# Second attention's scores as whole-array products of stacked high and low parts, and three adaLN maps moved to the feed-forward parts

## The chip, the cores and the metric

The kernel runs on one core of one Trainium2 chip (trn2). The metric is the device time of one execution in microseconds. Five engines work side by side: TensorE multiplies matrices (its weight loads are shown as an engine of their own), VectorE and ScalarE work elementwise and read the results out of PSUM, GpSimd helps with elementwise work, and SyncE (SP) issues the DMA transfers.

## The reference, cut to what matters

A trunk of two layers over 1024 latent tokens and 256 context tokens, width 1024, 16 heads of 64. Layer 0 mixes tokens by neighbourhood attention, layer 1 by sliding-window attention with 4 key and value heads (each serves 4 query heads), rotary positions and a sink logit for each head. Each layer ends with a gated feed-forward part with a convolution. Shift, scale and gate vectors ("adaLN maps", six for each layer, here v = 0 to 5) come from the condition vectors through one linear map.

```python
mod = silu_c @ w_mod[i] + b_mod[i]
sh1, sc1, gt1, sh2, sc2, gt2 = jnp.split(mod[:, None, :], 6, axis=-1)   # v = 0 .. 5
h = modulate(rmsnorm(x, g_attn[i]), sh1, sc1)
...
q = apply_rope(q, cos, sin)
k = apply_rope(k, cos, sin)
...
# sliding window: 128 queries see at most 384 latent keys (|i - j| <= 128) and all 256 context keys
s = jnp.einsum('...qngd,...knd->...ngqk', q, k) * (HEAD_DIM ** -0.5)
s = jnp.where(mask, s, NEG_INF)           # and a sink column
p = jax.nn.softmax(s, axis=-1)
...
x = x + gt1 * (o @ w_out)
h = modulate(rmsnorm(x, g_ffn[i]), sh2, sc2)
x = x + gt2 * conv_ffn(h, ...)
```

Layer 1 needs six maps for the latent tokens (r = 0) and only v = 0 and 1 for the context (r = 1), since the context's stream ends there.

## The kernel before, in words

Everything is float32. Large products are made as three products of the faster float32r kind, with each operand split in a high part (rounded by ScalarE) and a low part (the rest, by VectorE or GpSimd): high by high, low by high, high by low. A few products are made in plain float32.

The program is made stage by stage: first attention, its output projection, first feed-forward part (`ffn(0, ...)`), second attention, its output projection, second feed-forward part (`ffn(1, ...)`). In each stage a planner (`Sched`, line 61) is given operations with an engine (or two to choose from), an estimated duration, what they read and write, a key (smaller is earlier), and buffers to acquire and release (`caps` says how many there are of each kind). It simulates the engines and writes down the order of each engine's instructions; on the chip every engine then works strictly in that order. A key is a rank and no time to start. With `near=3.0` TensorE, after an operation marked as half-array ("t"), prefers another such one that is up to 3 keys later.

The second attention (from line 2326) works in four groups g of key and value heads. For each group, `plan_sw_qkv` makes for each tile tt of 128 tokens the projection (24 products of 384 columns), copies it out (`qraw`), normalises the heads, applies the rotation (`qn`, `qa`, `qb`, the last on GpSimd), transposes three 128x128 blocks into one PSUM bank ("pt"), and copies these out: two blocks of queries (each has two heads on 64 partitions each) into a tile `q`, and one block with the key head twice (on both halves of the partitions) into `kkl1`. Its key is 1.6 per tile, 16 per group. The context's keys go into `kkc1` in the same way (`plan_sw_ctx`). All of these are plain float32.

`plan_sw_su` then makes the attention for 128 queries j and a pair pr of heads, 64 such units in all. `plan_row_qk` multiplies 64 partitions of `q` with 64 partitions of the keys, for both heads side by side: the two heads lie on the two halves of TensorE's rows ("64*128" tiles in the profile). It acquires four PSUM banks of kind "s" at once: context scores and window scores of both heads; there are four. `plan_su` takes the scores' minimum against sink and mask on VectorE, the exponential on ScalarE, scales, transposes the probabilities ("pt" banks again) and copies them out; `plan_pv` multiplies with V for two pairs of heads at a time, in half-array tiles by columns ("128*64"). `plan_su` can also make its scores with `plan_split_qk`, as the first attention does: the operands are stacked, with the high part of a head's queries on one half of the partitions and the low part on the other, against keys that are held twice (high parts in one tile, low parts in another), so that two products over all 128 partitions make the whole score.

PSUM has eight banks here: 4 "s", 2 "pt", 2 "mm".

The maps of layer 1: `plan_mod1` (line 350), called in the first feed-forward part, makes v = 0 and 1 for both r. Each of its 64 dots (8 blocks x 2 maps x 2 r x 2 halves of the row) loads 128x512 of the weights into the one `mh` buffer (line 2033) and makes a dot on VectorE (`wmh` in the profile) with the c row, of which ScalarE makes a copy for each r and half. `plan_modv` (line 396), called in the second attention for v = 2 to 5, makes a dot of 128x1024 for each of 32 blocks (`wmt`), at keys 20 + 1.2 n.

`Oproj` (line 806) makes the output projection: `split` the high and low parts of the attention's output (`o0hi`, `o0lo` for the first 512 tokens, `o1hi`, `o1lo` for the rest), `weights` those of the weights, `project` the products. All wait (`gate`) for the projections of all eight tiles of the last group, as their buffers are those of the normalised input. `plan_oproj1` loads the residual x into the two buffers that held the context's normalised input (`hchi`, `hclo`).

Of the kernel before, what the change touches and what calls it, by code (L numbers as in the profile page):

```python
# [223 lines left out]
def trunk_kernel(ctx, tc, xtok, xseq, cc, crow, wmod, wmodt, bmod, gnorm, na_wqkv, na_gqk, na_bias, na_wo,  # L224
# [125 lines left out]
    def plan_mod1(sc, tile_, bank, key, step):  # L350

        crow = {}
        for r in range(2):
            for half in range(2):
# [10 lines left out]
                sc.op("act", t_actp(512), cp, reads=[ck + ("t",)], writes=[ck], key=key, acq=[("b", ck + ("p",), 2 * KT)], rel=[ck])  # L365
                for v in range(2):
                    for jt in range(KT):
                        st = {}
                        m = ("mh", r, v, jt)
                        raw = ("mh", r, half, v, jt)  # L370

# [6 lines left out]
                        def dot(e, st=st, r=r, half=half, v=v, jt=jt):  # L378
                            k = 24 + (2 * r + v) * KT + jt
                            a, b = small[:, k:k + 1], modc[:, 1, r, v, jt:jt + 1]  # L380
# [3 lines left out]
                        sc.op("dve", 0.7, dot, reads=[raw + ("here",), ck] + ([m + (0,)] if half else []), writes=[m + (half,)],  # L384
                              key=key, rel=[raw, ck + ("p",)])
                        key += step
        for v in range(2):
            def fin_(e, v=v):
                if v:
                    for r in range(2):  # L390
                        dve.scalar_tensor_tensor(out=modc[:, 1, r, v, :], in0=modc[:, 1, r, v, :], scalar=1.0, in1=gn[:, 1, 0, :],
                                                 op0=ALU.add, op1=ALU.mult)
            sc.op(*(("dve", 0.3) if v else ("x", 0.0)), fin_, reads=[("mh", r, v, jt, 1) for r in range(2) for jt in range(KT)],
                  writes=[("modc", v)], key=key)
# [140 lines left out]
    def plan_row_qk(sc, key, I, get, nl, psa, reads, rel):  # L535
        J = {}

        def mm(e):
            for h in range(2):
                J["sc", h], J["sl", h] = psa("s", F32), psa("s", F32)  # L540
            u = get()
            for t, x, n in (("sc", "kkc", TC), ("sl", "kk", nl)):
                for h in range(2):
                    a = slice(h * DH, h * DH + DH)
                    pe.matmul(J[t, h][:, :n], u["q"][a], u[x][a], start=True, stop=True)
        out = [I + (t, h) for h in range(2) for t in ("sc", "sl")]
        sc.op("pe", 0.207 + (TC + nl) * 4 / 2400.0, mm, kind="t", reads=reads, writes=out, key=key, acq=[("s", x, 1) for x in out],
              rel=rel)
        return J, I

    def plan_su(sc, key, I, units, groups, psa, wk, reads=()):
# [4 lines left out]
        if "s" not in units[0]:  # L556
            plan_split_qk(sc, key, J, K, units, psa, reads)
        for k in range(2):
            nl, sink = units[k]["nl"], units[k]["sink"]
            n = TC + nl  # L560
            if "s" in units[k]:
                Q, QI, hh = units[k]["s"]
                kc, kl, c0 = QI + ("sc", hh), QI + ("sl", hh), 0
                src_c, src_l = (lambda Q=Q, hh=hh: Q["sc", hh]), (lambda Q=Q, hh=hh: Q["sl", hh])
            else:
                kc, kl, c0 = K("sc"), K("sl", k), k * 256
                src_c, src_l = (lambda: J["sc"]), (lambda k=k: J["sl", k])
# [238 lines left out]
    class Oproj:  # L806
# [14 lines left out]
        def split(self, c, name, n, src, dst, key, reads, rel):  # L821
# [8 lines left out]
            g = self.c_gate if c == 2 else self.gate  # L830
# [23 lines left out]
        def project(self, dt, key, parts, evac):  # L854
# [3 lines left out]
            for kt in range(KT):  # L858
# [8 lines left out]
                sc.op("pe", 3 * t_pe(n), mm, reads=[("woh", dt), ("wol", dt)] + parts[kt] + self.gate, writes=[I], key=key,  # L867
# [494 lines left out]
    SRB, GB, MOD1 = 4, 3, 160  # L1362
# [3 lines left out]
    def ffn(l, opj, xt1, todo):  # L1366
# [665 lines left out]
        if not last:  # L2032
            plan_mod1(sc, lambda nm: fp.tile([P, 512], F32, tag="mh", name=nm, bufs=1), bank, MOD1, (KD - 120 - MOD1) / 64)
# [135 lines left out]
        def plan_ev(d, m, c, k, key, end=False):  # L2169
# [3 lines left out]
                reads=[("dn", d, m)], writes=[("xn", c, k)], key=key,  # L2173
# [157 lines left out]
    psa = ps_alloc(ps)  # L2331
    crow1 = fin.tile([P, D], F32, name="crow1")
    kkl1 = fin.tile([P, 2, T], F32, name="kkl1")
# [3 lines left out]
    PVT, SBUFS = "pt", 6  # L2337
    sc = Sched(dict(CAPS, pt5=6, pt2=3, qsq=1, q=10, S=SBUFS, s=4, qraw=3, qa=3, qn=3), near=3.0)
# [4 lines left out]
    KC = fin.tile([P, NKV, TC], F32, name="kkc1")  # L2343
    VC = [fin.tile([P, NKV, DH], F32, name=f"vc1{i}") for i in range(2)]

    def plan_sw_ctx(tt, key):
# [44 lines left out]
        sc.op("pe", 0.44, tr, reads=[K("k2")], writes=[K("pt")], key=key, acq=[("pt", K("pt"), 1)], rel=[K("k2")])  # L2391

        def kev(e):
            copy(e, KC[:, :, c * P:(c + 1) * P], J["pt"].rearrange("p (g k) -> p g k", g=NKV))
        sc.op(("act", "dve"), (t_actp(512), t_dve(512)), kev, reads=[K("pt")], writes=[("kC", c)], key=key, rel=[K("pt")])

    def plan_sw_qkv(n):
        g, tt = n // NT, ORDER[n % NT]
        key = n / NT * 16 + QKEY1
# [3 lines left out]
        nh, c0 = 5, 0  # L2403
# [3 lines left out]
        def cp(e):  # L2407
            J["raw"] = wk.tile([P, 384], F32, tag="qraw", name="qraw", bufs=3)
# [13 lines left out]
        def qn(e):  # L2422
            J["qn"] = wk.tile([P, 5, DH], F32, tag="qn", name="qn", bufs=3)
# [271 lines left out]
```

## Time and profile before

| | |
|---|---|
| median of 3 runs | 2730.73 us (2729.62 to 2731.26) |
| the profiled execution | 2731.01 us, span 2729.2 us |
| TensorE granted clock | 0.995 |
| second attention, about | 1604 to 2014 us of the span |
| score products in it | 1634.3 to 2002.0 us |
| dots of `plan_mod1` | 64, from 725.9 to 1286.8 us |
| dots of `plan_modv` in the second attention | 32, from 1662.2 to 1911.7 us |

Times in the profile are microseconds from the first instruction. A busy share is the share of time in which an engine has at least one instruction at work; TensorE's products overlap, and their ends are modelled, so the distance between two starts tells more than a length. A row of the timeline has the start, the length, the engine, the line (here always that of the helper that issues everything, L51), the operation, result and operands, the tile of the array and the shape, and how many there were. A row of one tile has the count, minimum, median and maximum duration in ns, first and last start, and the forms of a sample.

### The profile page before, as it was taken

How to read it: one execution, taken by the hardware profiler on the slowest of the kernel's cores; microseconds unless marked ns; L12 is line 12 of the kernel's file. 1: busy time of each engine (PE TensorE's matmuls, PEld its weight loads, DVE VectorE, ACT ScalarE, POOL GpSimd, SP SyncE). 2: the span in 40 equal slices, each digit the busy share in tenths (PEclk: the TensorE clock that was granted, in tenths of full speed). 3: DMA queues.
4: the chain of work that ended last, by engine and by line, in shares of the span. 5: the costliest groups of instructions: out<-in, count | busy, mean ns of one | idle time of the engine just before them, and what ended most of it. 6: DMA issues, size and time to landing. Idle time of an engine off the chain costs nothing. (4 is left out here: it accounts for less than half of the span.)

```text
span 2729.2 us, 42690 instructions
## 1 busy us (share of the span) xinstructions
PE 2680.4 (98%) x15168; PEld 2277.0 (83%) x15168; DVE 2290.8 (84%) x5063; ACT 1691.4 (62%) x3001; POOL 356.2 (13%) x520
## 2 busy tenths in 40 slices
PE   7999999999999999999999999999999999999999
PEld 5999999988899988888888887777678788888887
DVE  5988888888788899898886889899867988888767
ACT  6777777776455565656664557776654765656443
POOL 1211111122000000000010026455510000000000
PEclk8999999999999999999999999999999999999999
DMA  7343343344656744344475642233243233334655
GB/s 265 97 122 121 117 136 110 105 136 151 245 188 215 230 145 135 122 145 140 143 248 165 205 144 72 63 107 103 90 147 108 89 116 107 109 109 148 232 176 189
DMA packets 167005, 395.23 MB, mean 145 GB/s; under 512 B 36996, under 2 KB 44164, under 8 KB 166408
## 3 DMA queue, kind: packets, MB, share of 16 engines
q1 hardware_dynamic: 166792, 392.51, 44.1%
q8 instruction: 119, 1.95, 0.3%
q14 instruction: 94, 0.77, 0.1%
HBM read 325.46 MB, written 66.99 MB: 144 GB/s over the span
## 5 line engine op out<-in xcount | busy, mean ns | idle before, releaser
L51 ACT ACTIVATE whi<-wraw 128x512 fp32r<-128x512 f32 (+1 forms) x264 | 212.5, 805 | 148.3 <-PE uc L51 53.5
L51 DVE TENSOR_TENSOR wlo<-wraw,whi 128x512 fp32r<-128x512 f32 (+1 forms) x264 | 241.5, 915 | 33.5 <-ACT whi L51 31.5
L51 ACT ACTIVATE S<-S,m 128x640 f32<-128x640 f32 (+3 forms) x288 | 220.9, 768 | 68.2 <-DVE m L51 47.3
L51 PE MATMUL dn<-ghi,whi 128*128 128x512 f32 x616 | 240.0, 390 | 0.0
L51 PE MATMUL dn<-ghi,wlo 128*128 128x512 f32 x616 | 239.7, 389 | 0.0
L51 PE MATMUL dn<-glo,whi 128*128 128x512 f32 x616 | 239.7, 389 | 0.0
L51 ACT ACTIVATE whi<-s 128x1024 fp32r<-128x1024 f32 (+1 forms) x118 | 111.0, 942 | 182.6 <-PE uc L51 117.0
L51 POOL TENSOR_TENSOR qy<-qv,mhalf 128x4 f32<-128x4 f32 (+1 forms) x114 | 134.9, 1185 | 560.7 <-DVE qv L51 527.5
L51 PE MATMUL pt<-idr,S 128*128 128x128 f32 x1288 | 194.1, 278 | 14.1 <-DVE S L51 7.2
L51 PEld LDWEIGHTS pt<-idr,S 128*128 128x128 f32 x1288 | 151.5, 142 | 51.6 <-issue 11.8
L51 ACT ACTIVATE ghi<-graw 128x512 fp32r<-128x512 f32 x154 | 95.8, 629 | 142.2 <-PE dn L51 95.7
L51 ACT ACTIVATE pt<-pt 128x512 f32<-128x512 f32 (+2 forms) x263 | 136.5, 540 | 73.9 <-PE pt L51 72.0
L51 PE MATMUL mm<-whi,h0hi 128*128 128x384 f32 x512 | 179.9, 351 | 0.0
L51 PE MATMUL mm<-wlo,h0hi 128*128 128x384 f32 x512 | 172.0, 336 | 0.0
L51 DVE TENSOR_TENSOR glo<-graw,ghi 128x512 fp32r<-128x512 f32 x154 | 106.4, 699 | 73.4 <-ACT ghi L51 43.0
L51 DVE TENSOR_TENSOR wlo<-s,whi 128x1024 fp32r<-128x1024 f32 (+1 forms) x118 | 127.0, 1079 | 14.1 <-ACT whi L51 13.6
L51 PEld LDWEIGHTS dn<-ghi,whi 128*128 128x128 f32 x616 | 115.6, 188 | 24.3 <-issue 0.2
L51 PEld LDWEIGHTS dn<-glo,whi 128*128 128x128 f32 x616 | 115.6, 188 | 24.0
L51 PEld LDWEIGHTS dn<-ghi,wlo 128*128 128x128 f32 x616 | 115.6, 188 | 23.9
L51 PE MATMUL ua<-t12hi,whi 128*128 128x512 f32 x344 | 134.4, 391 | 0.9 <-ACT c L51 0.9
L51 PE MATMUL ua<-t12lo,whi 128*128 128x512 f32 x344 | 133.9, 389 | 0.0
L51 PE MATMUL ua<-t12hi,wlo 128*128 128x512 f32 x344 | 133.9, 389 | 0.0
(370 smaller groups left out, 8353.7 us busy)
## 6 DMA issues: line engine op xcount, KB each, us to landing
wraw<-in_w_up_dram SPq DMA_DIRECT2D x133, 512.0 KB, 3.8
wmt<-in_wmodt_dram SPq DMA_DIRECT2D x96, 512.0 KB, 4.1
wraw<-in_w_down_dram SPq DMA_DIRECT2D x44, 512.0 KB, 3.8
graw<-g_dram SPq DMA_DIRECT2D x44, 512.0 KB, 4.5
wraw<-in_w_down_dram SPq DMA_DIRECT2D x88, 256.0 KB, 3.1
graw<-g_dram SPq DMA_DIRECT2D x66, 256.0 KB, 2.8
wmh<-in_wmodt_dram SPq DMA_DIRECT2D x64, 256.0 KB, 3.3
slab<-in_na_wqkv_dram SPq DMA_DIRECT2D x32, 384.0 KB, 3.1
```

Source lines behind the costliest of these rows:

```text
L51: r = f(*a, **k)
```

## The change

1. Scores: `plan_row_qk` goes; `plan_sw_su` uses `plan_split_qk`. So queries and keys of this layer are split. `q` becomes four blocks (one for each head) with high and low parts on the two halves of the partitions, made by two ScalarE and two VectorE operations; the keys become `kkl1` and `kll1`, `kkc1` and `klc1`, by one ScalarE and one VectorE operation each. The transposes' bank is released after six readers instead of two.
2. Room: `q` has 5 buffers (8 uses) instead of 10 (2 uses). `qraw`, `qn` and `qb` move into the two buffers of the context's normalised input (`ring`), and the residual's load waits for the last group's transposes.
3. Keys: tile tt of group g has 16 g + 2 tt + 2.6 instead of 16 g + 1.6 (tt + 2).
4. Maps: v = 3 and 4 (r = 0) of layer 1 are made in the first feed-forward part by `plan_mod1`, which now takes a list of jobs: 96 dots of half a row instead of 64, from key 120 instead of 160 to the same end. v = 5 is made in the second feed-forward part: 16 dots. Only v = 2 stays in the second attention: 8 whole-row dots instead of 32.
5. Output projection of layer 1: the first half's `split` and the products wait for four tiles' projections instead of eight; the second half's splits for the other four.

```diff
-    def plan_mod1(sc, tile_, bank, key, step):
+    def plan_mod1(sc, tile_, bank, jobs, key, end):
-        crow = {}
-        for r in range(2):
+        crow, part = {}, {}
+        step = (end - key) / sum(2 * KT * len(vs) for _, vs in jobs)
+        for r, vs in jobs:
...
-                for v in range(2):
+                for v in vs:
...
-        if "s" not in units[0]:
-            plan_split_qk(sc, key, J, K, units, psa, reads)
+        plan_split_qk(sc, key, J, K, units, psa, reads)
...
-                for k in (2,) if c == 2 else (0, 1):
+                for k in (c,) if c == 2 or self.l else (0, 1):
...
-            g = self.c_gate if c == 2 else self.gate
+            g = self.c_gate if c == 2 else self.gate[4 * c:4 * c + 4] if self.l else self.gate
...
-    SRB, GB, MOD1 = 4, 3, 160
+    SRB, GB, MOD1 = 4, 3, 120
...
-        if not last:
-            plan_mod1(sc, lambda nm: fp.tile([P, 512], F32, tag="mh", name=nm, bufs=1), bank, MOD1, (KD - 120 - MOD1) / 64)
+        mh = lambda nm: fp.tile([P, 512], F32, tag="mh", name=nm, bufs=1)
+        plan_mod1(sc, mh, bank, *(([(0, [5])], KU + 100, KD - 120) if last else ([(0, [0, 1, 3, 4]), (1, [0, 1])], MOD1, KD - 120)))
...
-    kkl1 = fin.tile([P, 2, T], F32, name="kkl1")
+    kkl1, kll1 = [fin.tile([P, 2, T], F32R, name=nm) for nm in ("kkl1", "kll1")]
...
-    PVT, SBUFS = "pt", 6
-    sc = Sched(dict(CAPS, pt5=6, pt2=3, qsq=1, q=10, S=SBUFS, s=4, qraw=3, qa=3, qn=3), near=3.0)
+    PVT, SBUFS, QB1 = "pt", 6, 5
+    sc = Sched(dict(CAPS, pt5=6, pt2=3, qsq=1, q=QB1, S=SBUFS, s=4, qraw=3, qa=3, qn=3), near=3.0)
...
+    AREA = {}
+    def ring(i, a, n, bufs, m):
+        if i not in AREA:
+            AREA[i] = hpool.tile([P, 2048], F32, tag=("hchi", "hclo")[i], name=f"ring{i}", bufs=1)
+        return AREA[i][:, a + m % bufs * n:a + m % bufs * n + n]
...
-        key = n / NT * 16 + QKEY1
+        key = 16 * g + 2 * tt + 2.6 + QKEY1
...
-              acq=[("pt", K("pt"), 2)], rel=[K("a")])
-        kk = ("kk", g % 2, tt)
-        def kev(e):
-            copy(e, kkl1[:, g % 2, tt * P:(tt + 1) * P], J["pt"][:, 2 * P:3 * P])
-        sc.op(("act", "dve"), (t_actp(128), t_dve(128)), kev, reads=[K("pt")], writes=[kk], key=key, rel=[K("pt")])
-        def qev(e):
-            q = f["q"][tt] = fin.tile([P, 2, P], F32, tag="q", name="q", bufs=10)
-            copy(e, q.rearrange("p a b -> p (a b)"), J["pt"][:, :2 * P])
+              acq=[("pt", K("pt"), 6)], rel=[K("a")])
...
+        for x in range(2):
+            def qhi(e, x=x):
+                if x == 0:
+                    f["q"][tt] = fin.tile([P, 4, P], F32R, tag="q", name="q", bufs=QB1)
+                act.activation(qt(x, x), qp(x), AF.Copy)
+            def qlo(e, x=x):
+                dve.tensor_tensor(out=qt(1 - x, x), in0=qp(x), in1=qt(x, x).bitcast(F32), op=ALU.subtract)
...
-    for n in range(4 * KT):
+    for n in range(KT):
         plan_modv(sc, 1, 0, 2 + n // KT, n % KT, wmodt[1, 2 + n // KT, n % KT], lambda: crow1, MKEY + MSTEP * n, [("crow1",)])
...
-            sc.op("dma", 3.2, load, reads=op1.gate, writes=[("xc", k)], key=OKEY + k)
+            sc.op("dma", 3.2, load, reads=op1.gate + [("q1", NKV - 1, t, "pt") for t in range(8)], writes=[("xc", k)],
+                  key=OKEY + k)
```

More of the change, by code (lines that the diff above doesn't have):

```diff
@@ L533, in plan_split_qk @@
                       acq=[("s", K("sl", k), 1)], rel=units[k]["rel_l"])
[L535 to L549, printed above, removed]
     def plan_su(sc, key, I, units, groups, psa, wk, reads=()):
@@ L2342, in trunk_kernel @@
     SLAB0 = (("dve", "pool"), (0.87, 1.75))
-    KC = fin.tile([P, NKV, TC], F32, name="kkc1")
+    KC, KL = [fin.tile([P, NKV, TC], F32R, name=nm) for nm in ("kkc1", "klc1")]
     VC = [fin.tile([P, NKV, DH], F32, name=f"vc1{i}") for i in range(2)]
@@ L2436, in qb @@
         def qb(e):
[L2437 removed]
+            J["b"] = ring(0, 1152, 320, 2, nt).rearrange("p (h d) -> p h d", d=DH)
             for k, s, m in spans:
@@ L2479, in plan_sw_su @@
         nl, m0 = (hi - lo + 1) * P, P if j == 0 else 0
-        Q = plan_row_qk(sc, key, I, lambda: dict(q=f["q"][j][:, pr, :], kkc=KC[:, g, :], kk=kkl1[:, g % 2, ks]), nl, psa,
-                        [("q", g, j), ("kC", 0), ("kC", 1)] + [("kk", g % 2, t) for t in range(lo, hi + 1)], [("q", g, j)])
+        reads = [("q", g, j, x, z) for x in range(2) for z in range(2)] + [(n, c) for n in ("kC", "kD") for c in range(2)]
+        reads += [(n, g % 2, t) for n in ("kk", "kl") for t in range(lo, hi + 1)]
         for k in range(2):
@@ L2485, in get @@
             def get(hd=hd):
-                return dict(mask=bandt[:, m0:m0 + nl], sink=sink[:, 4 * g + hd:4 * g + hd + 1])
-            units.append(dict(nl=nl, sink=1, get=get, mask_key=[], s=Q + (k,)))
+                return dict(q=f["q"][j][:, hd, :], kkc=KC[:, g, :], klc=KL[:, g, :], kk=kkl1[:, g % 2, ks], kl=kll1[:, g % 2, ks],
+                            mask=bandt[:, m0:m0 + nl], sink=sink[:, 4 * g + hd:4 * g + hd + 1])
+            units.append(dict(nl=nl, sink=1, get=get, mask_key=[], rel_c=[("q", g, j)], rel_l=[("q", g, j)]))
         lst = [(8 + i, i * P, i * P) for i in range(2)] + [(b, *[TC + (b - lo) * P] * 2) for b in range(lo, hi + 1)]
@@ L2490, in plan_sw_su @@
                for t, a, b in lst]
-        f["half", pr] = plan_su(sc, key, I, units, [lst[i:i + 2] for i in range(0, len(lst), 2)], psa, wk)
+        f["half", pr] = plan_su(sc, key, I, units, [lst[i:i + 2] for i in range(0, len(lst), 2)], psa, wk, reads)
         if pr == 0:
@@ L2561, in plan_oproj1 @@
                 key = OKEY + 6 * (c - 1) + kt
-                sc.op("dma", 1.0, load, reads=[("od", kt // 2, 2 * c + i) for i in range(2)] + op1.gate, writes=[r], key=key, acq=[("raw", r, 2)])
+                sc.op("dma", 1.0, load, reads=[("od", kt // 2, 2 * c + i) for i in range(2)] + op1.gate[4 * c:4 * c + 4], writes=[r], key=key, acq=[("raw", r, 2)])
                 op1.split(c, (c, kt), 512, lambda c=c, kt=kt: R[c, kt][:, :512], lambda a, kt=kt: a[:, kt, :], key + 0.5, [r], [r])
```

74 lines of the change are left out of this document (45 added, 29 removed).

## The prediction

> **What bounds the kernel now.** I read the page first, then the busy times by stage, then who waited for whom on TensorE, then TensorE's timeline.
>
> ```profile
> span 2729.2 us, 42690 instructions
> PE 2680.4 (98%) x15168; PEld 2277.0 (83%) x15168; DVE 2290.8 (84%) x5063; ACT 1691.4 (62%) x3001; POOL 356.2 (13%) x520
> ```
>
> ```profile
> 850.00:950.00 100.00, 100.00 (x836) 100.00 (x835) 79.02 (x138) 54.14 (x81) 0.00 (x0) 1.00 0.74 232
> 1000.00:1300.00 300.00, 300.00 (x1325) 248.50 (x1324) 269.28 (x354) 181.83 (x215) 0.00 (x0) 1.00 0.40 135
> 1604.00:2014.00 410.00, 397.36 (x2681) 306.30 (x2681) 363.18 (x1195) 282.30 (x611) 219.88 (x400) 0.99 0.28 88
> 2150.00:2550.00 400.00, 399.31 (x1762) 330.32 (x1761) 334.41 (x395) 244.57 (x303) 0.00 (x0) 1.00 0.39 131
> ```
>
> The stage rows give TensorE, its weight loads, VectorE, ScalarE and GpSimd, then the granted clock. The first two rows lie in the first feed-forward part, the third is the second attention, the fourth is in the second feed-forward part. TensorE is at work without a hole in the feed-forward parts. In the second attention it stands idle for 410.00 - 397.36 = 12.6 us, and VectorE works for 363.2 of the 410. So the whole kernel goes at TensorE's pace: time is won where TensorE's stream gets shorter, and lost only where a wait opens in it. TensorE's own waits in the second attention, the three largest:
>
> ```profile
> PE pt L51 <- DVE S L51: 3.8, 4, 1.8
> PE pt L51 <- POOL qa L51: 3.5, 4, 1.3
> PE pt L51 <- ACT o0hi L51: 2.4, 1, 2.4
> ```
>
> They are single late arrivals in an order fixed beforehand, not one engine that is always late.
>
> **The score products.** All score products of this layer, first by count, then one stretch of TensorE's timeline (start, length, how many):
>
> ```profile
> L51 PE MATMUL s<-kkc,q x256: 376/480/793, 1634.3 to 2001.6; 64*128 64x256 f32 x128
> L51 PE MATMUL s<-kkl,q x256: 376/482/845, 1634.8 to 2002.0; 64*128 64x384 f32 x96, 64*128 64x256 f32 x32
> ```
>
> ```profile
> 1701.99 0.81 PE L51 MATMUL pt<-idr,S 128*128 128x128 f32 x6
> 1702.57 0.42 PE L51 MATMUL mm<-whi,h1hi 128*128 128x384 f32 x1
> ...
> 1704.52 0.33 PE L51 MATMUL mm<-whi,h1lo 128*128 128x384 f32 x1
> 1704.69 0.34 PE L51 MATMUL mm<-wlo,h1hi 128*128 128x384 f32 x1
> 1704.96 0.70 PE L51 MATMUL s<-kkc,q 64*128 64x256 f32 x4
> 1705.49 0.81 PE L51 MATMUL s<-kkl,q 64*128 64x384 f32 x4
> 1706.24 1.08 PE L51 MATMUL pt<-pt,vc 128*64 128x256 f32 x8
> ...
> 1709.13 0.70 PE L51 MATMUL s<-kkc,q 64*128 64x256 f32 x4
> 1709.67 0.60 PE L51 MATMUL s<-kkl,q 64*128 64x256 f32 x4
> 1710.20 0.87 PE L51 MATMUL pt<-idr,S 128*128 128x128 f32 x6
> 1710.83 0.42 PE L51 MATMUL mm<-whi,h1hi 128*128 128x384 f32 x1
> ```
>
> Four entries a pair of heads make 256 / 4 = 64 units; the forms (a sample, 96 to 32) say that three quarters, 48, have a window of 384 keys and 16 one of 256. The lengths overlap, so I price by the distance between starts. A unit with 384 keys takes 1706.24 - 1704.96 = 1.28 us, one with 256 takes 1710.20 - 1709.13 = 1.07. Around a unit lies more: the projection ahead of it takes 1704.96 - 1704.69 = 0.27 where its neighbour takes 0.17, so 0.10 to enter half-array tiles; and the six transposes behind one take 1710.83 - 1710.20 = 0.63 where six behind a projection take 1702.57 - 1701.99 = 0.58, so 0.05 after it. A unit that stands alone costs 1.43 or 1.22 us.
>
> The new form stands in this trace already: the first attention has it, with the same sizes.
>
> ```profile
> 308.39 0.28 PE L51 MATMUL s<-kkc,q 128*128 128x256 f32 x1
> 308.50 0.28 PE L51 MATMUL s<-klc,q 128*128 128x256 f32 x1
> ...
> 308.86 0.28 PE L51 MATMUL s<-kkl,q 128*128 128x256 f32 x1
> ...
> 309.09 0.34 PE L51 MATMUL s<-kkl,q 128*128 128x384 f32 x1
> 309.27 0.34 PE L51 MATMUL s<-kll,q 128*128 128x384 f32 x1
> 309.45 0.33 PE L51 MATMUL mm<-whi,h0hi 128*128 128x384 f32 x1
> ```
>
> Four products over the 256 context keys take 308.86 - 308.39 = 0.47, so 0.118 each; one over 384 takes 309.45 - 309.27 = 0.18. The projection follows at once: there is no entry and no exit, as these are whole-array products like their neighbours. A new unit costs 4 x 0.118 + 4 x 0.177 = 1.18 us, or 8 x 0.118 = 0.94. That is 0.25 (384) or 0.28 (256) less than a unit alone.
>
> Not all stand alone. In TensorE's timeline from the first to the last score product, 25 of the 64 (21 with 384 keys, 4 with 256) lie beside a product with V, as the one at 1704.96. That product works in half-array tiles as well, stays so, and then has to pay the entry (0.10) and the 0.05 itself. There the gain is 0.25 - 0.15 = 0.10, or 0.13. Sum: 27 x 0.25 + 12 x 0.28 + 21 x 0.10 + 4 x 0.13 = 12.7 us. The bounds: 64 x 0.10 = 6.4 if all stood beside such a product, 48 x 0.25 + 16 x 0.28 = 16.5 if none did. The new order of work will shift the count, so the range has to hold some of this.
>
> A rule of the Trainium skill speaks against the change: "TensorEngine Tiling (Array Packing)", Overview, puts two-row tiling for contractions of up to 64 at up to twice the speed, and the change gives that tiling up. By that rule alone the scores would take up to twice as long as now. The rows above decide otherwise: the whole-array unit took 1.18 us against 1.28.
>
> **The operands for them.** Per latent tile two evacuations (queries, keys) become six: high part of each half of the queries on ScalarE, its low part on VectorE, and the same once for the keys. The nearest rows are the same operations of the first attention, and the ones that go.
>
> ```profile
> L51 DVE TENSOR_TENSOR kll<-pt,kkl x64: 416/422/430, 74.2 to 638.3; 64x256 fp32r<-64x256 f32 x64
> L51 ACT ACTIVATE kkl<-pt x80: 255/366/383, 70.0 to 1973.9; 64x256 fp32r<-64x256 f32 x64, 128x128 f32<-128x128 f32 x16
> L51 DVE COPY kkl<-pt x16: 274/291/292, 1645.1 to 1957.5; 128x128 f32<-128x128 f32 x16
> L51 DVE COPY q<-pt x16: 398/415/426, 1664.1 to 1974.2; 128x256 f32<-128x256 f32 x16
> L51 ACT ACTIVATE q<-pt x16: 361/379/387, 1632.1 to 1909.0; 128x256 f32<-128x256 f32 x16
> L51 DVE CUSTOM_DVE_ANT_0 wmt<-wmt,crow,bmod_t x32: 1259/1278/2464, 1662.2 to 1911.7; 128x1024 f32<-128x1024 f32 x32
> ```
>
> VectorE gains 64 x 0.422 = 27.0 us for the queries and 32 x 0.29 = 9.3 for the keys (the 128x128 copy is the nearest; 0.42 at most, 13.4), and loses 16 x 0.415 + 16 x 0.291 = 11.3. It also loses 24 of the 32 dots of the adaLN maps, 24 x 1.278 = 30.7. Net 27.0 + 9.3 - 11.3 - 30.7 = -5.7 us: 363.2 becomes about 358, and the longest blocks on its queue are gone. ScalarE gains 64 x 0.366 + 32 x 0.27 - 16 x (0.379 + 0.27) = 21.7 us, 282 to 304 of some 400. Both stay below TensorE's load, so I put this at 0 on the path. What it does cost is time to arrival: a tile's PSUM bank (two serve all transposes and products with V) is held by three pairs of ScalarE and VectorE operations instead of two copies, about 3 x 0.37 + 0.3 = 1.4 us instead of 0.7 to 0.8, and the score products wait for all six. That is the second rival's matter.
>
> **The order of work.** The score unit takes its PSUM banks in three steps (context, then each head) instead of four at once, which lets the next unit's first products start earlier. Queries have 5 buffers instead of 10, and the tiles' keys lie 2 apart instead of 1.6, so the projections come nearer to their use. The old buffers' place is lent by the context's tiles, dead after the first projections. The output projection's high and low parts for the first half wait for four tiles instead of eight, so they spread into the attention. Today they bunch at its end, where TensorE waits longest:
>
> ```profile
> 1970.93 1.28 PE L51 MATMUL pt<-idr,S 128*128 128x128 f32 x7 [2.42 <-ACT o0hi L51]
> ```
>
> I take this one wait, 2.4 us, as won and leave the other 10.2 us as they are. Bounds: all 12.6 us go, or they double (+12.6), since the order of everything in the stage is new.
>
> **The dots that move.** 32 more half-row dots in the first feed-forward part (96 instead of 64), 16 in the second, each with its 256 KB load on SP's queue, with 2 more loads and ScalarE copies of the c row. Their price is known:
>
> ```profile
> L51 DVE CUSTOM_DVE_ANT_0 wmh<-wmh,crow,bmod_t x32: 736/742/768, 725.9 to 1175.2; 128x512 f32<-128x512 f32 x32
> ```
>
> 48 x 0.742 = 35.6 us on VectorE, 23.7 and 11.9. What hides them: TensorE's stream without a hole, and VectorE's idle time, 21.0 us in 850 to 950 alone, 30.7 in 1000 to 1300, 65.6 in 2150 to 2550. The first feed-forward part's 23.7 us spread over 820 to 1300, by their keys; in the 400 us of it that the stage rows show, VectorE's idle time sinks from 51.7 to about 51.7 - 23.7 x 400 / 480 = 32 us. I take 0.5 us; if nothing covered them, 35.6.
>
> **Sum.** The profiled execution took 2731.0 us (2729.2 between first and last instruction, 1.8 around it), 0.3 above the median of the runs. 2731.0 - 12.7 - 2.4 + 0.5 = **2716.4 us**.
>
> **The rivals.** About 0.2%, 5.5 us, is what a measurement of this kernel can tell from no change: faster is below 2725.3, slower above 2736.2.
>
> *The freed time turns into waiting* (0.13). If VectorE's chain (scores, minimum, scaling) sets the pace of a unit, TensorE does less and waits more, and only the tail and a few microseconds come off: 2726 to 2731, say 2729. For it: the wait on DVE S is TensorE's largest. Against it: VectorE's load falls, and it worked 89% where TensorE worked 97%.
>
> *The query tiles come too late* (0.09), the case on the slower side. Place: the transposes of a tile and the bank that they fill. With keys 2.9 ahead of their scores, half the buffers and six operations instead of two, each of the 32 tiles could make TensorE wait. The longer hold alone is 0.7 us, and a wait on both the bank and the scores at each tile costs 1.4: 32 x 1.4 = 45 us against 14.6 won, 2761; it passes no change at 14.6 / 32 = 0.46 us a tile and the slower bound at 0.62; a little above that, 0.8, gives 2742. For it: TensorE waits 3.5 us for GpSimd's part of just this chain now. Against it: those are 4 waits in 32 tiles, and the dots, one of 1.3 us often ahead of a chain's step, are gone.
>
> *The waits nearly vanish too* (0.08): with the banks taken in steps and no dots, 8 to 12 us of idle time go as well: about 2708.
>
> *Full-array products at half speed* (0.01): doubling 48 x 1.28 + 16 x 1.07 = 78.6 us of scores gives 2810. This is the skill's tiling rule as a mechanism here; the first attention's rows leave it hardly a chance.
>
> **How the numbers follow.** My forecast, 2710 to 2724, has 0.69. Faster: 0.69 + 0.08 = 0.77; within 0.2%: 0.13, and 0.01 from the query tiles' mild case, so 0.14; slower: 0.08 + 0.01 = 0.09. The range runs from 2706 (the waits vanish, or more units stand alone than now) to 2729 (the freed time turns into waiting). It leaves out the two slow cases and the far ends of the others.
>
> **What would show it.** Right: score products as 128*128 forms, 512 in all and 118 and 177 ns apart; about 32 stretches of half-array work, those with V alone; the second attention some 15 us shorter with TensorE's idle time at about 10 us; the feed-forward parts as long as now and still without a hole, with 96 and 16 dots of 0.74 us. Wrong: an idle time of over 20 us in the second attention, waits on the query and key operands or on the transposes' banks; gaps in the first feed-forward part after 820 us by VectorE; the second attention as long as now with TensorE less busy.

## The result, and the profile after

The changed kernel takes 2715.8 us (median of 4 runs, 2714.9 to 2716.95) against 2730.89 us (4 runs, 2729.62 to 2731.26): a ratio of 0.9943, 95% interval 0.9932 to 0.9955, so 15.1 us less. The prediction said 2716.4, in 2706 to 2729. The profiled execution took 2716.95 us, 14.1 less than the one of before, and it is that difference which the rows below divide up.

The first two lines of the page of the changed kernel:

```profile
span 2715.2 us, 42914 instructions
PE 2669.4 (98%) x15168; PEld 2301.8 (85%) x15168; DVE 2326.1 (86%) x5205; ACT 1696.6 (62%) x3039; POOL 336.5 (12%) x520
```

TensorE issues the same 15168 products in 11.0 us less; VectorE has more work than before, not less. To see where the 14.0 us of the span went, I divide both traces at the same three events: the first product of the first feed-forward part's context, the first projection of the second attention, and the first product of the second half's output projection. (In the kernel before the first event comes at 766.45 us; its first row starts 0.75 us ahead of that.) The rows have the stretch, its length, then busy times and counts of TensorE, weight loads, VectorE, ScalarE, GpSimd, then the clock, the DMA share and GB/s. First the kernel before:

```profile
765.70:1605.10 839.40, 836.42 (x4457) 725.30 (x4456) 730.68 (x1084) 489.37 (x683) 13.35 (x11) 1.00 0.54 175
1605.10:2043.00 437.90, 425.26 (x2802) 329.33 (x2801) 376.64 (x1208) 291.92 (x623) 219.52 (x400) 0.99 0.30 94
2043.00:2729.20 686.20, 680.25 (x3009) 561.34 (x3007) 547.26 (x723) 372.85 (x502) 2.02 (x2) 1.00 0.41 138
```

Then the changed kernel:

```profile
765.60:1604.30 838.70, 835.79 (x4453) 724.63 (x4453) 748.10 (x1150) 491.82 (x683) 13.20 (x11) 1.00 0.58 185
1604.30:2028.00 423.70, 413.40 (x2802) 355.33 (x2801) 382.58 (x1252) 293.61 (x659) 198.62 (x400) 1.00 0.21 68
2028.00:2715.20 687.20, 680.86 (x3009) 561.12 (x3007) 559.41 (x755) 373.71 (x504) 2.03 (x2) 1.00 0.44 144
```

The second row of each, which I call the middle stage below (second attention and the first half of its output projection), is 437.9 - 423.7 = 14.2 us shorter. TensorE's work in it falls by 425.26 - 413.40 = 11.9 us, its idle time from 12.6 to 10.3 us, by 2.3. The first feed-forward part, with 32 dots more, is as long as before (838.7 us from the event itself in both); the last stretch, with 16 dots more, is 1.0 us longer.

Not all of such a difference means something. Three kernels of the experiments below (`e14_no_near`, `e15_old_estimate`, `e6_double_dots`, in this order) give TensorE the same order of products in the middle stage as the changed kernel:

```profile
1604.00:2026.10 422.10, 411.81 (x2802) 353.94 (x2801) 382.80 (x1252) 293.63 (x659) 198.32 (x400) 1.00 0.21 68
1610.30:2032.50 422.20, 411.88 (x2801) 353.91 (x2800) 382.81 (x1252) 292.70 (x658) 198.72 (x400) 1.00 0.21 67
1652.70:2077.40 424.70, 414.94 (x2801) 357.04 (x2800) 383.11 (x1252) 293.64 (x659) 198.40 (x400) 0.99 0.21 68
```

With the changed kernel's own 423.7 and 413.4, one order has lengths from 422.1 to 424.7 us and TensorE's work from 411.8 to 414.9; its idle time is 10.3, 10.3, 10.3 and 9.8 (in two more pairs with one order of TensorE's, e1 and e5, e9 and e13, it differs by 1.4 and 1.0). So in one profile a stage's length or TensorE's work is known to some 2 to 3 us, and idle time is the steadier number. The last stretch varies from 686.1 to 688.5 us in the four kernels without the 16 dots (before, e1, e5, e12) and from 686.4 to 688.2 in the nine with them (the changed kernel, e2, e3, e4, e7, e9, e13, e14, e15), so its 1.0 us is no price of theirs.

The score products of the changed kernel's second attention, one of their four groups of 128 (`kkc`, `klc`, `kkl`, `kll`; 512 in all), and then a stretch of TensorE's timeline:

```profile
L51 PE MATMUL s<-kkl,q x128: 278/344/668, 1637.5 to 1986.1; 128*128 128x384 f32 x96, 128*128 128x256 f32 x32
```

```profile
1763.71 0.42 PE L51 MATMUL s<-kkl,q 128*128 128x384 f32 x1
1763.97 0.34 PE L51 MATMUL s<-kll,q 128*128 128x384 f32 x1
1764.15 0.33 PE L51 MATMUL s<-kkl,q 128*128 128x384 f32 x1
1764.32 0.34 PE L51 MATMUL s<-kll,q 128*128 128x384 f32 x1
1764.49 0.34 PE L51 MATMUL mm<-whi,h1hi 128*128 128x384 f32 x1
```

Only whole-array forms are left, and products over 384 keys lie 0.17 to 0.18 us apart (1764.49 - 1764.15 = 0.34 for two), with the projection straight behind them. Only the first, which stands behind transposes, holds TensorE for 0.26 (1763.97 - 1763.71). The stretches of half-array work, counted in TensorE's timeline, are 32, all of products with V, where before there were 71.

TensorE's waits in the middle stage of the changed kernel, the four largest, and the one long hole in its timeline:

```profile
PE pt L51 <- DVE kll L51: 2.8, 2, 2.5
PE pt L51 <- ACT S L51: 2.3, 2, 1.2
PE pt L51 <- DVE pt L51: 1.7, 3, 0.9
PE pt L51 <- DVE S L51: 1.4, 3, 0.9
```

```profile
1948.28 0.44 PE L51 MATMUL pt<-idr,S 128*128 128x128 f32 x2 [2.47 <-DVE kll L51]
```

The waits for GpSimd's part of the rotation (3.5 us before) and for the output projection's high part (2.4 us) are gone. In their place stands one that did not exist: 2.5 us for VectorE's low part of the keys, the last of the six operations that now hold a tile's bank.

### The profile page after: what moved, and what is told of

The parts are those of the page before. It is cut to its first block, busy times and chain, and to the rows that moved or that the text cites. A ratio compares the mean times of both kernels' runs of the same rounds, so it can differ in the third digit from the quotient of the medians.

```text
span 2715.2 us, 42914 instructions
## 1 busy us (share of the span) xinstructions
PE 2669.4 (98%) x15168; PEld 2301.8 (85%) x15168; DVE 2326.1 (86%) x5205; ACT 1696.6 (62%) x3039; POOL 336.5 (12%) x520
```

## The experiments

Every kernel ran beside the kernel before on the same chip; medians, and ratios with 95% intervals. My theory at the outset was the prediction's: the shorter score stream and the earlier output projection make the gain, and the moved dots neither help nor harm. Its rival was that VectorE's relief from the 24 long dots makes part of it.

### Each half alone

`e1_scores_only` has the scores, the room, the keys and the output projection's order of the change, and all maps where they were:

```diff
-    SRB, GB, MOD1 = 4, 3, 120
+    SRB, GB, MOD1 = 4, 3, 160
-        plan_mod1(sc, mh, bank, *(([(0, [5])], KU + 100, KD - 120) if last else ([(0, [0, 1, 3, 4]), (1, [0, 1])], MOD1, KD - 120)))
+        if not last:
+            plan_mod1(sc, mh, bank, [(0, [0, 1]), (1, [0, 1])], MOD1, KD - 120)
-    for n in range(KT):
+    for n in range(4 * KT):
         plan_modv(...)
```

> The changed kernel with the adaLN maps left where they were: 64 half-row dots in the first feed-forward part from key 160, none in the second, 32 whole-row dots in the second attention. My theory (the score products' shorter stream is the gain, the moved dots only keep VectorE from taking it back): TensorE's work in the stage falls by 12 us as in the changed kernel, but VectorE would be busy for some 390 us of a stage of 400, so 5 to 12 us of it come back as idle time of TensorE: 2719 to 2727, say 2722. Rival (the moved dots are the gain): 2728 or more, no faster than before by 0.2%.

Measured: 2732.65 us against 2731.1, ratio 1.0009 (1.0 to 1.0018): no gain at all, the rival's number and not my 2719 to 2727. Its stages, in the order of those above (the last one 688.50):

```profile
764.50:1609.10 844.60, 838.84 (x4454) 725.58 (x4452) 727.99 (x1082) 489.96 (x683) 11.39 (x10) 1.00 0.54 173
1609.10:2042.60 433.50, 416.02 (x2801) 355.18 (x2802) 397.04 (x1266) 308.03 (x693) 219.94 (x405) 1.00 0.31 96
```

The middle stage is 4.4 us shorter, but the first feed-forward part is 5.9 us longer than before (844.6 against 838.7 from the same event), though it has the very same dots. One thing in it differs: the change also raises the planner's estimate of a half-row dot from 0.70 to 0.75 us, which the list of the change above leaves out. The next kernel takes that back.

```diff
-                        sc.op("dve", 0.75, dot, ...
+                        sc.op("dve", 0.7, dot, ...
```

> The scores-only kernel with the planner's old estimate of 0.70 us for a half-row dot instead of 0.75, so that the first feed-forward part is ordered as in the kernel before. In the scores-only run that part took 5.7 us longer than before, with waits on VectorE near its end, though it does the same work. Theory (the order that the planner happens to find did that): the 5.7 us go, the second attention stays 4 us shorter than before: 2726 to 2728. Rival (the stacked scores cost something outside their stage): 2731 or more.

Measured (`e5_scores_old_estimate`, the line above on top of e1): 2725.51 us against 2731.03, ratio 0.9978 (0.9969 to 0.9987), just below my range. The first feed-forward part is 838.5 us again. Its middle stage, and TensorE's largest wait there:

```profile
1603.50:2035.20 431.70, 415.59 (x2802) 354.99 (x2802) 396.48 (x1263) 307.81 (x693) 220.13 (x405) 1.00 0.31 96
```

```profile
PE pt L51 <- DVE sm L51: 4.2, 3, 2.5
```

The scores alone take 9.7 us of work from TensorE, but its idle time grows from 12.6 to 16.1 us, with VectorE at 396.5 of 431.7 us: 6.2 us shorter in all. By the medians the estimate alone was worth 7 us; 6.1 us of difference lie in the first feed-forward part, whose order it sets and which the scores don't touch.

`e2_maps_only` is the other half: the kernel before with change 4 alone, the maps moved, and with it the new estimate of a dot.

```diff
-                        sc.op("dve", 0.7, dot, ...
+                        sc.op("dve", 0.75, dot, ...
...
-    SRB, GB, MOD1 = 4, 3, 160
+    SRB, GB, MOD1 = 4, 3, 120
...
+        plan_mod1(sc, mh, bank, *(([(0, [5])], KU + 100, KD - 120) if last else ([(0, [0, 1, 3, 4]), (1, [0, 1])], MOD1, KD - 120)))
...
-    for n in range(4 * KT):
+    for n in range(KT):
         plan_modv(...)
```

> The kernel before with its scores, buffers and keys, and only the adaLN maps moved to the feed-forward parts. My theory: TensorE's work stays, and its idle time of 12.6 us in the second attention falls by 3 to 6 us, since the 1.3 us dots leave VectorE's queue; the feed-forward parts take at most 1 us more: 2725 to 2728. Rival (the moved dots are the gain): 2716 to 2720.

Measured: 2724.83 us against 2731.1, ratio 0.9978 (0.9968 to 0.9987), just below my range. Its middle stage:

```profile
1605.10:2035.50 430.40, 421.89 (x2802) 329.57 (x2802) 355.55 (x1177) 283.95 (x612) 199.62 (x392) 0.99 0.21 67
```

437.9 - 430.4 = 7.5 us shorter with the old scores; idle time 8.5 us instead of 12.6. The other 3.4 us are TensorE's work, 421.9 instead of 425.3, which I had expected to stay; the products are the same, and half-array stretches 69 instead of 71. That is hardly more than one order varies by, and its cause is open. So the rival holds beside the theory. In the middle stage the halves nearly add: 6.2 + 7.5 = 13.7 of 14.2 us, to the 2 or 3 us of single profiles. By the medians they bring 5.5 and 6.3 of the 15.1; the remaining 3.3 us these runs don't settle (e5's profiled execution was 2.4 us below its median, and two measurements of the changed kernel, see e14, lie 1.5 apart).

### Parts of the new order

`e3_old_keys` gives the tiles their old keys; `e4_old_gates` lets the whole output projection wait for all eight tiles again.

```diff
-        key = 16 * g + 2 * tt + 2.6 + QKEY1
+        key = n / NT * 16 + QKEY1
```

> The changed kernel with the old keys of the projections, 1.6 a tile instead of 2. My theory: keys only shift which work waits; within 3 us of the changed kernel, 2713 to 2719. Rival (the new spacing is needed with 5 query buffers, as early tiles find no buffer and hold a transposes' bank): 5 us or more above it, 2721 and up.

Measured: 2722.25 us, ratio 0.997 (0.996 to 0.9981) against before, so 6.4 us above the changed kernel: the rival's number, not my 2713 to 2719. The middle stage, and TensorE's two largest waits in it:

```profile
1604.00:2033.10 429.10, 413.73 (x2801) 355.36 (x2800) 388.78 (x1245) 296.61 (x664) 201.22 (x402) 1.00 0.21 67
```

```profile
PE pt L51 <- DVE S L51: 5.2, 6, 1.4
PE s L51 <- DVE m L51: 2.4, 4, 0.8
```

TensorE works as long as in the changed kernel (413.7 and 413.4) and stands idle for 15.4 us instead of 10.3. The new keys belong to the new scores: without them the waits on VectorE's probabilities are larger than before the change. That the five buffers of queries cause it was only argued.

```diff
-            g = self.c_gate if c == 2 else self.gate[4 * c:4 * c + 4] if self.l else self.gate
+            g = self.c_gate if c == 2 else self.gate
-                sc.op("pe", 3 * t_pe(n), mm, reads=[("woh", dt), ("wol", dt)] + parts[kt] + (self.gate[:4] if self.l else self.gate), ...
+                sc.op("pe", 3 * t_pe(n), mm, reads=[("woh", dt), ("wol", dt)] + parts[kt] + self.gate, ...
-                sc.op("dma", 1.0, load, reads=[...] + op1.gate[4 * c:4 * c + 4], ...
+                sc.op("dma", 1.0, load, reads=[...] + op1.gate, ...
```

> The changed kernel with the output projection of the second attention waiting for all eight tiles again, for its splits and its products. My theory: the wait at the stage's end comes back, 2 to 3 us: 2718 to 2719, with TensorE idle at the end of the attention on the first half's high parts. Rival (the gates do nothing, the wait went for another reason): 2715 to 2716.5.

Measured: 2719.28 us, ratio 0.9958 (0.9945 to 0.997), 3.5 us above the changed kernel. The middle stage is 425.7 us, idle time 12.9 instead of 10.3 (+2.6). TensorE's largest wait after 1930 us:

```profile
PE pt L51 <- POOL qa L51: 1.9, 2, 1.5
```

The size is the predicted 2.4, but the wait is another: not one for `o0hi`, which never comes back, but GpSimd's part of the tiles' rotation. The wait for `o0hi` is also gone in e2 and e12, which keep the old gates, so the gates weren't its cause alone.

`e7_banks_at_once` takes all three score banks of a unit at its start, as the old score products took their four.

```diff
             J["sc"] = psa("s", F32)
+            if once:
+                for k in range(2):
+                    J["sl", k] = psa("s", F32)
...
-              acq=[("s", K("sc"), 2)], ...
+              acq=[("s", K("sc"), 2)] + ([("s", K("sl", k), 1) for k in range(2)] if once else []), ...
```

> The changed kernel with a score unit of the second attention acquiring its three PSUM banks at once, ahead of its first product, instead of one by one. Theory (the step-wise banks keep TensorE fed): 2 to 6 us more idle time, 2718 to 2722. Rival (banks were no limit): 2714 to 2717.5.

Measured: 2716.02 us, ratio 0.9944 (0.9931 to 0.9958), the changed kernel's own time. The middle stage is 422.2 us, TensorE's idle time 11.3, about as in the changed kernel. Taking the banks in steps brings nothing that shows.

Two kernels drop the planner's preference for half-array work beside half-array work (`near`), one on the kernel before, one on the changed kernel. The first was to price a mode change by itself, with the old scores.

```diff
-    sc = Sched(dict(CAPS, pt5=6, pt2=3, qsq=1, q=10, S=SBUFS, s=4, qraw=3, qa=3, qn=3), near=3.0)
+    sc = Sched(dict(CAPS, pt5=6, pt2=3, qsq=1, q=10, S=SBUFS, s=4, qraw=3, qa=3, qn=3), near=0.001)
```

> The kernel before, with the planner no longer preferring a second half-array operation behind a first one (near 0.001 instead of 3), so that fewer score units stand beside a product with V. Theory (every stretch of half-array work costs TensorE 0.15 us of entry and exit beyond what two neighbours share): more stretches than 71, up to 96, and 0.15 us more TensorE work for each one more, up to 4 us; its idle time may shift by a few us either way. Rival (entries and exits cost nothing): TensorE's work in the stage unchanged within 0.5 us.

Measured: 2729.93 us against 2731.74, ratio 0.9993 (0.9983 to 1.0003): no difference. Its middle stage:

```profile
1604.00:2039.40 435.40, 427.93 (x2802) 329.23 (x2801) 379.78 (x1213) 287.43 (x619) 208.90 (x399) 1.00 0.30 95
```

Half-array stretches are 81 instead of 71, TensorE works 427.93 - 425.26 = 2.7 us longer, 0.27 for each stretch more if all of it is theirs, and stands idle 5.2 us less. As one order varies by as much, the run agrees with 0.15 a stretch but doesn't price it. An order free of the preference wins the difference back in waits.

```diff
-    sc = Sched(dict(CAPS, pt5=6, pt2=3, qsq=1, q=QB1, S=SBUFS, s=4, qraw=3, qa=3, qn=3), near=3.0)
+    sc = Sched(dict(CAPS, pt5=6, pt2=3, qsq=1, q=QB1, S=SBUFS, s=4, qraw=3, qa=3, qn=3), near=0.001)
```

> The changed kernel without the planner's preference for half-array work behind half-array work. Only the 32 products with V are of that kind now, so there is little left to put together. Theory: 32 stretches as before, TensorE's work the same within 0.5 us, and 5 us less idle time as in the kernel before only if the preference itself made TensorE wait; I expect within 3 us of the changed kernel, 2713 to 2718. Rival (the preference holds back projections and transposes behind each product with V): 2708 to 2712.

Measured: 2714.3 us (2713.62 to 2717.14) against 2731.58, ratio 0.9937 (0.9924 to 0.9949). It is the lowest time of all, and yet it is the changed kernel: with only products with V left in half-array tiles the preference decides nothing, and the planner writes the same instructions in the same order for every engine. So 2715.8 and 2714.3 us, 15.1 and 17.3 below the kernel before, are two measurements of one program, and a difference of 2 us between runs tells nothing.

### The dots that moved

`e6_double_dots` follows each moved dot with a second VectorE operation of the same size, whose result nobody reads.

```diff
                                                      accum_out=b if half else a)
+                            dve.tensor_tensor(out=st["raw"], in0=st["raw"], in1=crow[r, half], op=ALU.mult)
-                        sc.op("dve", 0.75, dot, ...
+                        sc.op("dve", 1.35, dot, ...
```

> The changed kernel with a second VectorE operation of the same size behind each half-row dot in the feed-forward parts (its result is used by nobody), planned at 1.35 us instead of 0.75: some 58 us more on VectorE in the first part, 10 in the second. Theory (the moved dots are free as long as VectorE has idle time, 44 us from 820 to 1300): the first part becomes VectorE's by 10 to 25 us, the second stays: 2726 to 2741. Rival (TensorE's lead hides any such work there): 2716 to 2719.

Measured: 2765.16 us against 2731.03, ratio 1.0129 (1.0115 to 1.0143), 49 us above the changed kernel and far above my 2726 to 2741 (the profiled run is 6 us above this median). The first feed-forward part, the added operations in it, and TensorE's largest wait there:

```profile
764.40:1652.70 888.30, 852.43 (x4454) 730.33 (x4453) 805.89 (x1241) 492.49 (x683) 12.90 (x11) 0.98 0.54 174
```

```profile
L51 DVE TENSOR_TENSOR wmh<-wmh,crow 128x512 f32<-128x512 f32 x91 | 62.5, 687 | 3.1
```

```profile
PE ua L51 <- DVE wlo L51: 19.3, 8, 6.9
```

62.5 us of added work made the stage 888.3 - 838.7 = 49.6 us longer, although VectorE had stood idle there for 838.7 - 748.1 = 90.6 us. Its busy time rose by 57.8 us (operations overlap a little) and its idle time fell to 82.4, so some 8 of the 90.6 took up added work. Of the 49.6, 852.4 - 835.8 = 16.6 us are TensorE at work for longer on the same products, at a mean granted clock of 0.98, and the rest are waits; what the clock and the waits have to do with each other the run doesn't tell. Nor does it part the added work from what comes with it: a new order (the estimate is higher) and a longer hold of the `mh` buffer. Still, an engine's idle time is no measure of what it can take: the weights' low parts, which TensorE waits for, are made on the same queue.

`e9_all_maps` goes one step further than the change: the last map left in the attention, v = 2, moves too, 16 dots more in the first feed-forward part.

```diff
-([(0, [0, 1, 3, 4]), (1, [0, 1])], MOD1, KD - 120)
+([(0, [0, 1, 2, 3, 4]), (1, [0, 1])], MOD1, KD - 120)
-    for n in range(KT):
-        plan_modv(sc, 1, 0, 2 + n // KT, ...)
```

> The changed kernel with the last map (v = 2) moved to the first feed-forward part as well: 112 dots there, none in the second attention. Theory (what VectorE is freed of in the second attention shortens it, and the first part still has cover): 8 x 1.28 = 10 us less on VectorE there, 1 to 4 us less in all, 2712 to 2715. Rival (8 dots are too few to matter, or the first part is full now): 2715 to 2720.

Measured: 2757.97 us against 2731.03, ratio 1.0095 (1.0081 to 1.0109), 42 us above the changed kernel, for 16 x 0.742 = 12 us of work, and outside both ranges. Where it goes stands in TensorE's timeline: the first product of the down projection, then one long wait (the bracket has the idle time ahead and what ended it) and the next products. Behind them stand the last two dots in VectorE's timeline, and then the middle stage.

```profile
1382.00 0.47 PE L51 MATMUL dn<-ghi,whi 128*128 128x512 f32 x1
...
1437.52 0.80 PE L51 MATMUL dn<-ghi,whi 128*128 128x512 f32 x1 [38.23 <-DVE modc L51]
1438.11 0.63 PE L51 MATMUL dn<-glo,whi 128*128 128x512 f32 x1
1438.54 0.63 PE L51 MATMUL dn<-ghi,wlo 128*128 128x512 f32 x1
```

```profile
1433.19 0.75 DVE L51 CUSTOM_DVE_ANT_0 wmh<-wmh,crow,small 128x512 f32<-128x512 f32 x1 [2.58 <-DMA wmh<-in_wmodt_dram]
1436.71 0.75 DVE L51 CUSTOM_DVE_ANT_0 wmh<-wmh,crow,small 128x512 f32<-128x512 f32 x1 [2.76 <-DMA wmh<-in_wmodt_dram]
```

```profile
1648.40:2069.30 420.90, 411.72 (x2801) 355.63 (x2800) 374.86 (x1243) 292.55 (x653) 190.80 (x398) 1.00 0.18 57
```

The copy of the c row lies in a PSUM bank and keeps it until the last dot. The down projection needs all eight banks: 75 of its products run in the other seven from 1382.0 us on, and the 76th, the first into the eighth bank, waits 38.2 us for that dot. Behind the wait the next products lie 0.43 us apart (1438.54 - 1438.11) until 1441.1 us, where they take 0.23 otherwise. And the dots can't hurry: the one `mh` buffer is loaded, used and loaded again, 3.5 us a dot (1436.71 - 1433.19), of which VectorE works 0.75. In the changed kernel the last dot starts at 1362.2 us, 17.6 ahead of the down projection's first product (1379.8); in the kernel before it was 1286.8. How far the cliff is from there depends on the order too, since the planner can put the product that needs the last bank later (in e13 below it does). The middle stage is 2.8 us shorter than the changed kernel's, little more than one order varies by. A second `mh` buffer wasn't tried.

`e13_all_maps_early` lets the same 112 dots begin earlier.

```diff
-    SRB, GB, MOD1 = 4, 3, 120
+    SRB, GB, MOD1 = 4, 3, 40
```

> The kernel with all maps in the first feed-forward part, its dots keyed from 40 instead of 120. In the run with all maps TensorE stood still for 38 us at the turn to the down projection, until the last dot: the down projection's accumulators need all eight PSUM banks, and the copy of the c row holds one until the dots are done. Theory (that edge is the cost): the last dot comes some 30 to 60 us earlier than 1437, and the wait shrinks by as much, to 0 to 10 us; the second attention stays 3 us shorter than in the changed kernel; 2713 to 2728 in all. Rival (VectorE is overfull in that part, wherever the dots lie): 2745 and up.

Measured: 2718.7 us against 2731.74, ratio 0.9954 (0.9939 to 0.9969), 39 us below e9. Its last dots, and its first feed-forward part:

```profile
L51 DVE CUSTOM_DVE_ANT_0 wmh<-wmh,crow,small x56: 739/742/750, 968.2 to 1396.9; 128x512 f32<-128x512 f32 x56
```

```profile
767.80:1611.90 844.10, 838.44 (x4454) 726.15 (x4454) 757.88 (x1178) 491.13 (x683) 13.39 (x11) 1.00 0.58 187
```

The last dot starts at 1396.9 instead of 1436.7, in time although that is 11.5 us behind the down projection's first product (1385.4): the wait for the bank is gone, and with it 37.9 of the 43.3 us by which e9's part was longer. That part is still 844.1 us, 5.4 more than in the changed kernel, while the middle stage (420.2) gains 3.5. All maps moved is no better than the change's choice.

`e15_old_estimate` is the changed kernel with the old estimate of a dot, the edit of e5.

```diff
-                        sc.op("dve", 0.75, dot, ...
+                        sc.op("dve", 0.7, dot, ...
```

> The changed kernel with the planner's old estimate of 0.70 us for a half-row dot (it takes 0.74). With the maps left in place that estimate moved the first feed-forward part by some 6 us. Theory (only the order around the turn to the down projection is touched by it, by chance): 2714 to 2722, the last dot of the first part within 10 us of 1362. Rival (the new estimate is a needed part of the change): 2725 and up.

Measured: 2721.33 us against 2731.58, ratio 0.9961 (0.9948 to 0.9975), 5.5 us above the changed kernel. The first feed-forward part:

```profile
766.00:1610.30 844.30, 838.75 (x4453) 727.30 (x4452) 747.58 (x1150) 493.59 (x684) 13.40 (x11) 1.00 0.58 184
```

844.3 us again, the length of e1, though the last dot starts at 1363.4, only 1.2 us later than in the changed kernel. With 64 dots the estimate 0.70 gives the better order and 0.75 the worse; with 96 dots it is the other way round. Neither value is the better one: each gives another order of some 4450 products, and orders differ by 5 to 6 us in this stage. Why one order wins was not settled.

## Why the prediction was right, and which steps were not

**The score products: right in kind, too large in size, and helped by luck.** There are 512 whole-array forms, at the predicted spacing behind the first of a run, and 32 half-array stretches, and TensorE's work in the middle stage fell by 11.9 us where 12.7 were predicted. But the scores by themselves take off 9.7 us (before to e5) or 8.5 (e2 to the changed kernel); the 3.4 us by which the work falls when the maps move (e2) were not in the prediction and fill the gap. One step missing from its price of a unit is in the timeline above: 86 of the changed kernel's 102 runs of score products stand behind transposes, and the first product of such a run holds TensorE for 0.23 us on average, not 0.12 or 0.18. A projection behind transposes pays as well (0.26 against 0.17), so part of this has only moved; how much of the missing 3 us it makes is open. The finer split has limits anyway: TensorE's work lies between 410.1 us (e13) and 416.0 (e1) in the eleven kernels with these products and 32 stretches, and between 411.8 and 414.9 with one and the same order.

On the rule of the Trainium skill that the prediction weighed ("TensorEngine Tiling (Array Packing)", Overview: two-row tiling up to twice as fast), the traces decide as the first attention's rows did: giving the tiling up made the work shorter, 425.3 to 415.6 us with the maps in place (e5) and 421.9 to 413.4 with them moved (e2, changed kernel). As the products went from plain float32 to split float32r at the same time, this is no test of the rule for one kind of product.

**The operands, "0 on the path": wrong, in both of its halves, which nearly cancel.** The prediction had VectorE's load fall by 5.7 us and put that at nothing. Before and after, VectorE's groups in the middle stage:

```profile
L51 DVE TENSOR_SCALAR S<-S,sm 128x640 f32<-128x640 f32 (+1 forms) x81 | 46.9, 580 | 0.9
L51 DVE CUSTOM_DVE_ANT_0 wmt<-wmt,crow,bmod_t 128x1024 f32<-128x1024 f32 x32 | 45.3, 1417 | 0.0
```

```profile
L51 DVE TENSOR_SCALAR S<-S,sm 128x640 f32<-128x640 f32 (+1 forms) x100 | 62.7, 629 | 0.7
L51 DVE TENSOR_TENSOR q<-pt,q 64x256 fp32r<-64x256 f32 x64 | 27.0, 422 | 7.4 <-ACT kkl L51 4.0 <-ACT q L51 1.9
L51 DVE CUSTOM_DVE_ANT_0 wmt<-wmt,crow,bmod_t 128x1024 f32<-128x1024 f32 x8 | 10.2, 1276 | 0.0
```

The queries' low parts came to 27.0 us as predicted. The dots gave back 45.3 - 10.2 = 35.1 us rather than 30.7 (their mean was 1417 ns, and the prediction used the median, 1278). But the planner may choose the engine of the scaling, and put 19 more of these on VectorE, 15.8 us. So VectorE's load rose by 5.9 us in a stage 14.2 us shorter, and ScalarE's by 1.7 instead of 21.7. The value of it is not zero: with the scores alone TensorE waits 3.5 us more (e5, where its work falls by 9.7 and the stage by 6.2), and with the dots' leaving alone 4.1 us less (e2, 7.5 us off the stage). The sum came out by luck, as the waits that one half opens the other closes. That VectorE's load is what opens and closes them fits the largest wait of e5, on VectorE, but no run changes that load alone.

**The output projection's order, 2.4 us: right in size, by luck.** Undoing it costs 2.6 us of idle time (e4), but in other waits; the named one stays away with the old gates too (e2, e4, e12). And the changed kernel has a new wait of 2.5 us near the attention's end.

**"The other 10.2 us as they are": right as a sum (10.3 us), not as a list.** That the sum holds is luck as well. Of the three largest waits before, one remains, smaller (`DVE S`, 1.4 us instead of 3.8).

**The keys and the buffers, without a price: a gap.** The keys are worth 6.4 us to the new form (e3; 5.1 us of idle time): a part of the gain that the sum took for granted.

**The banks in steps: wrong.** They were to let the next unit start earlier; e7 shows no difference in time.

**The moved dots, 0.5 us: right, by the wrong cover and with luck.** Measured 0.0 in the first feed-forward part, and nothing that stands out of the noise in the last stretch. The prediction named VectorE's idle time and TensorE's stream without a hole as the cover (its own last row has 399.31 of 400 us, so not wholly without), and 35.6 us as the price without it. e6 shows that some 8 of 90.6 idle microseconds were taken up, and e9 that the risk was of another kind: a PSUM bank that the chain of dots holds, at 42 us for 16 dots more. A slower case of that sort was not among the rivals. And with the old estimate of a dot the same 32 dots go with a part that is 5.6 us longer (e15, 844.3 against 838.7), so that they came out free hangs on an order that nobody chose for it.

**The rivals.** The freed time did not turn into waiting (idle 10.3 us), though in e5, without the maps, a part of it did; nor did the waits vanish. The query and key tiles make TensorE wait 2.8 us in two places and 0.3 in a third, not at each of 32 tiles. Full-array products are not at half speed.

## What to carry to other kernels

An engine beside the bottleneck can have an idle share and still set the time: price its relief and its load by what waits for it, not by the sum of busy times, and undo each half alone, since two halves may hold each other up. Before moving work into a stage, look at what its chain holds (here a PSUM bank) and when the next step needs that back; such a margin is invisible until it is used up. Where an order is planned from estimates, a few microseconds (5 to 6 here) come and go with any edit, so a part's worth is read from the stage that it touches. And measure one program twice before reading 1 or 2 us: here a stage's length varied by 2.6 us with the order unchanged, its idle time by 0.5 (1.4 at most).

## What the runs showed of the hardware

A whole-row dot on VectorE holds up GpSimd. One stretch of GpSimd's timeline in the kernel before, and the dot at that time:

```profile
1702.40 1.30 POOL L51 COPY S<-small 128x1 f32<-128x1 f32 x2 [0.44 <-PE pt L51]
```

```profile
1702.26 1.28 DVE L51 CUSTOM_DVE_ANT_0 wmt<-wmt,crow,bmod_t 128x1024 f32<-128x1024 f32 x1
```

Two copies of one column, 0.18 us each at the median, took 1.30 and ended after the dot. All 128 of them, before and after:

```profile
L51 POOL COPY S<-small 128x1 f32<-128x1 f32 x128 | 36.2, 307 | 3.5 <-PE pt L51 2.6 <-POOL S L51 0.9
```

```profile
L51 POOL COPY S<-small 128x1 f32<-128x1 f32 x128 | 25.7, 230 | 0.0
```

The same 128 copies take 30.5 us in e5 and 28.9 in e12 (32 dots as before), 27.3 in e2 (8 dots as after) and 23.7 in e13 (none), so they go with the number of dots. GpSimd's whole busy time in the middle stage falls too: 219.5, 220.1 and 208.9 us with 32 dots (before, e5, e12), 198.6 and 199.6 with 8 (after, e2), 190.8 with none (e9). But its other operations differ from kernel to kernel, so these sums give no price of one dot. What on the chip the two share, the runs don't show.
